# Experts ordered by load, three of them on 64 slots, in a two-layer encoder on one core

## The chip, the core and the metric

The kernel runs on one core of a Trainium2 chip. The core has a tensor engine (PE, with its weight loads shown apart as PEld), a vector engine (DVE), a scalar engine (ACT), GpSimd (POOL), and a sync engine (SP) on whose queue all the loads of weights are issued. The metric is device time of one execution in microseconds. A trace shows each instruction of one profiled execution, with times counted from the start of its span.

## The reference

Layer 0 is a convolution and pooling mixer, cross-attention and a dense SwiGLU; layer 1 is a Conformer convolution, cross-attention and the experts, on which this case turns. There are 256 tokens of 1024 features, 8 experts with 3584 hidden features, and each token takes its two best experts:

```python
def moe_swiglu(xn, router, w_gu, w_down):
    logits = (xn @ router).astype(jnp.float32)
    top_v, top_i = lax.top_k(logits, TOP_K)
    w = jax.nn.softmax(top_v, axis=-1)
    comb = jnp.sum(jax.nn.one_hot(top_i, N_EXPERTS, dtype=jnp.float32) * w[..., None],
                   axis=-2).astype(xn.dtype)
    out = jnp.zeros_like(xn)
    for e in range(N_EXPERTS):
        out = out + comb[..., e:e + 1] * swiglu(xn, w_gu[e], w_down[e])
    return out
```

With the reference's own inputs the experts get 68, 72, 52, 68, 57, 70, 76 and 49 tokens.

## The kernel before

All of layer 0, and layer 1 up to its attention, keep activations transposed; the change leaves them alone. Float32 products run as three passes of float32r: each operand is split into a high part (12 significant bits) and its remainder, here hi and lo, and hi x hi, lo x hi and hi x lo are summed in PSUM.

The experts run one after the other, in their natural order. `Gather` fills 128 slots with an expert's tokens: a one-hot tile made on DVE (`one_hot`), the tokens picked out by float32 products (`gathered`, L1008), and both parts of the result in `xg` (L1028 on ACT, L1029 on DVE). The slots are the stationary operand (128 columns), the weights move past them 512 columns at a time. The weights come in chunks of 128 x 2048 float32 (1 MB), 42 of them for each expert. `split` makes both parts of a chunk in two halves of 1024 columns: ACT writes hi (L161), DVE subtracts and writes lo (L162). There are four buffers of a half for hi and four for lo (NPART), so that the split runs at most two chunks ahead of PE.

An expert has seven steps (`j`). A step takes six chunks, called here A0 and A1 (the gate, `gate_up(j, 0)`), B0 and B1 (up, `gate_up(j, 1)`), and D0 and D1 (`down` of the step before; the last step's own two come at the expert's end). `moving` does twelve products of 512 columns with each chunk: hi of the weights with both parts of the slots (L204, L205: eight), then lo with the slots' hi (L209: four). `gate` applies SiLU to the gate's sum on ACT (L1076) and multiplies it with up's on DVE (L1078, tile `eh`); `to_rows` turns `eh` on PE (L1084) and splits it into `ht` (L1086 on ACT, L1087 on DVE). At an expert's end `weighted` splits the output (L1100, L1101) and `scatter` adds it to the tokens' rows (L1108, L1109 on PE, L1111 on DVE).

SP loads the chunks in the order of their use (`sources`, `fetch`), from addresses known when the kernel is built, into a ring of 17 slots: 11 `raw`, 6 `spare`. A load waits until the chunk that had the slot has been split. The order of the instructions on PE, ACT and DVE within the experts is set when the kernel is built, by a scheduler with its own estimate of times; each engine then executes its list strictly in that order, and waits where an operand isn't there. Slots beyond 128 would be done by a second pass under a branch (`overflow`), which is not entered.

Of the kernel before, what the change touches and what calls it, by code (L numbers as in the profile page):

```python
# [42 lines left out]
CAP = 128  # L43
TCKW = dict(schedule_with_timeline_sim=True)
# [3 lines left out]
RING = "rrrrrrrrsssssrrrrrs"   # the slots of the experts' chunks, later ones as their forerunners  # L48
# [3 lines left out]
G_TAPS = 4 * (11, 12)  # of the convolution's 31 taps, on GpSimd  # L52

# columns of the packed per-partition vectors
# [20 lines left out]
def _build(ctx, tc, io, cap):  # L75
# [32 lines left out]
    # ---------------------------------------------------------------- inputs and constants  # L108
# [21 lines left out]
    for _ in range(NWARM):       # the tensor engine's clock rises with its load  # L130
        PE.matmul(idle[:, :P], ones, ones, start=True, stop=True)
# [3 lines left out]
    # ---------------------------------------------------------------- helpers  # L135
# [36 lines left out]
    class Early:  # L172
        """The same in two whole chunks for use much later, split piece by piece."""
# [69 lines left out]
    def product_whole(raw, act):  # L243
        """The same with float32 operands as they are."""
# [19 lines left out]
    def split_whole(name, t):  # L264
        """The two parts of a whole operand."""
# [14 lines left out]
    def rsqrt(out, v, n):  # L280
        """out = v ** -0.5 for [128, n]: an estimate from the bits, then a step of the second
        order and one of the third."""
# [4 lines left out]
        def half(y):  # L287
            """t = -v * y ** 2 / 2"""
# [13 lines left out]
    class Sums:  # L302
        """Sums over features, by pairs of feature tiles as they come: on GpSimd, and the last
        `last` pairs on the tensor engine."""
# [19 lines left out]
        def pair(self):  # L324
            """Adds the last two summed tiles, or the halves of the only one."""
# [6 lines left out]
        def columns(self):  # L332
            """[128 tokens, 2]"""
# [10 lines left out]
    def rstd(sums):  # L344
        """The columns [128 tokens, 2] of 1 / rms."""
# [7 lines left out]
    def broadcast(cols, name="rb", tag="rb", bufs=1, scale=1.0):  # L353
        """[128, T] with cols[t] times scale in every partition."""
# [87 lines left out]
    # ---------------------------------------------------------------- cross-attention  # L442
# [72 lines left out]
    # ================================================================ layer 0: mixer  # L515
# [15 lines left out]
    # reciprocals of the window sizes, clipped at both ends of the sequence  # L531
# [34 lines left out]
    def pool_evac(j, ps):  # L566
# [9 lines left out]
        # window sums by doubling: s[i] = u[i] + ... + u[i + width - 1]  # L576
# [50 lines left out]
    # ================================================================ layer 0: attention, SwiGLU  # L627
# [73 lines left out]
    # ================================================================ layer 1: Conformer  # L701
# [102 lines left out]
    # LayerNorm over features: the mean (in every partition), then the centred variance; what is  # L804
    # kept is the negative of the centred activations
# [35 lines left out]
    # ================================================================ layer 1: attention  # L841
# [24 lines left out]
    class Tokens:  # L866
        """Tokens on partitions, a quarter of the features: the experts' input without the 1 / rms."""
# [24 lines left out]

    def sources():
        """The experts' chunks, as they are used."""
        for e in range(NE):
            for j in range(7):
                for i in range(4):
                    yield io["moe_gu"][e, j, i], 1
                    if i == 3 and j:
                        for n in range(2):  # L900
                            yield io["moe_down"][e, j - 1, n], 1
            for n in range(2):
                yield io["moe_down"][e, 6, n], 4 if e == NE - 1 else 1
# [30 lines left out]
    # ================================================================ layer 1: router  # L934
    ltri = work.tile([P, NE, NE], F32, tag="w1", name="ltri", bufs=w1b)    # 1 where the other expert comes first
# [7 lines left out]
    upper = work.tile([P, P], F32, tag="w1", name="upper", bufs=w1b)      # [t', t] = 1 where t' < t  # L943
# [35 lines left out]
    # a token's slot: how many earlier tokens chose the expert  # L979
# [7 lines left out]
    # ================================================================ layer 1: experts  # L987
    def one_hot(e, first, n, dt):
        oh = work.tile([P, 2, P], dt, tag="sqs", name="oh")
        for t in range(2):  # L990
# [354 lines left out]
```

## Time and profile before

| | us |
|---|---|
| median of three runs | 1596.82 (1596.51 to 1597.1) |
| span of the profiled execution | 1595.4 |
| what lies around the span, taken as median less span | 1.4 |
| experts, first weights to the last product's end | 593.3 to some 1579 |
| PE, DVE and ACT busy in those 985.7 us | 985.70, 892.44, 753.17 |

The profile page gives busy time by engine and by forty slices of the span, the costliest groups of instructions, and the chain that ended last. Time of a product in the trace runs from its start to its modelled end and overlaps the next one, so the distance between two starts tells what a product costs PE. For DVE and ACT likewise: a run of n equal instructions is shown with the time from the first's start to the last's end.

### The profile page before, as it was taken

The numbers are of one execution on the slowest core, as the hardware profiler recorded it, in microseconds if no ns is written. First come the engines' busy times: TensorE is split into PE (matmuls) and PEld (weight loads), VectorE is DVE, ScalarE is ACT, GpSimd is POOL, SyncE is SP. The second block draws the span as 40 slices with busy tenths as digits, with TensorE's granted clock in tenths as the row PEclk, the third lists the DMA queues.
The fourth block names the chain that finished last, engine by engine and source line by source line (L and its number), as shares of the span: only waits on it lengthen the run. The fifth ranks groups of instructions, "written<-read, shape, count | busy, mean of one in ns | idle before, by whom it ended". The sixth has DMA issues, their size and how long they took to land.

```text
span 1595.4 us, 23969 instructions
## 1 busy us (share of the span) xinstructions
PE 1569.4 (98%) x8978; PEld 1383.1 (87%) x8978; DVE 1346.2 (84%) x1723; ACT 1087.7 (68%) x1384; POOL 148.6 (9%) x206
## 2 busy tenths in 40 slices
PE   8899999999999999999999999999999999999996
PEld 8899999999889998888888888888888888888885
DVE  7866677766998769989989999989999989889896
ACT  5555554455576548777777777777777777777775
POOL 4710100000592110000000000000000000000000
PEclk9999999999999999999999999999999999999998
DMA  9654454336436569999999998998998999999950
GB/s 370 249 187 161 154 185 152 117 127 240 185 132 236 188 237 347 364 348 337 379 360 340 378 364 326 376 369 325 373 369 322 374 362 342 358 359 353 349 195 29
DMA packets 65213, 451.44 MB, mean 283 GB/s; under 512 B 7360, under 2 KB 7488, under 8 KB 12480
## 3 DMA queue, kind: packets, MB, share of 16 engines
q1 hardware_dynamic: 65088, 449.83, 75.4%
q8 instruction: 72, 1.18, 0.3%
q14 instruction: 53, 0.43, 0.1%
HBM read 448.75 MB, written 1.05 MB: 282 GB/s over the span
## 4 chain that ended last, share of the span: by engine, by line
PE 89%; POOL 3%; DVE 3%; ACT 2%; issue 1%; DMA 1%; SPq 0%; POOLq 0%; DVEq 0%; ACTq 0%
PE gu L209 13%; PE gu L204 13%; PE gu L205 13%; PE acc L198 6%; PE acc L197 6%; PE acc L196 6%; PE py L209 6%; PE py L204 6%; PE py L205 6%; POOL part L757 2%; PE gx L1008 2%; PE ht L1084 2%; DVE lo L162 1%; PE acc L248 1%; PE lead L197 1%
## 5 line engine op out<-in xcount | busy, mean ns | idle before, releaser
L162 DVE TENSOR_TENSOR lo<-raw,hi 128x1024 fp32r<-128x1024 f32 (+2 forms) x599 | 703.8, 1207 | 117.8 <-ACT hi L161 95.0
L161 ACT CAST hi<-raw 128x1024 fp32r<-128x1024 f32 (+2 forms) x599 | 600.3, 1033 | 266.6 <-PE acc L197 92.4
L204 PE MATMUL gu<-hi,xg 128*128 128x512 f32 x896 | 350.1, 391 | 0.0
L205 PE MATMUL gu<-hi,xg 128*128 128x512 f32 x896 | 349.3, 390 | 0.0
L162 DVE TENSOR_TENSOR lo<-spare,hi 128x1024 fp32r<-128x1024 f32 (+1 forms) x242 | 281.9, 1202 | 27.1 <-ACT hi L161 15.2
L161 ACT CAST hi<-spare 128x1024 fp32r<-128x1024 f32 (+1 forms) x242 | 241.6, 1038 | 55.3 <-PE gu L205 41.5
L209 PE MATMUL gu<-lo,xg 128*128 128x512 f32 x896 | 251.6, 391 | 0.0
L204 PEld LDWEIGHTS gu<-hi,xg 128*128 128x128 f32 x896 | 168.2, 188 | 35.3
L205 PEld LDWEIGHTS gu<-hi,xg 128*128 128x128 f32 x896 | 168.3, 188 | 35.2
L209 PEld LDWEIGHTS gu<-lo,xg 128*128 128x128 f32 x896 | 167.7, 188 | 35.6
L204 PE MATMUL py<-hi,ht 128*128 128x512 f32 x448 | 175.7, 394 | 0.0
L205 PE MATMUL py<-hi,ht 128*128 128x512 f32 x448 | 174.9, 390 | 0.0
L209 PE MATMUL py<-lo,ht 128*128 128x512 f32 x448 | 136.1, 396 | 0.0
L205 PEld LDWEIGHTS py<-hi,ht 128*128 128x128 f32 x448 | 84.2, 188 | 16.8
L204 PEld LDWEIGHTS py<-hi,ht 128*128 128x128 f32 x448 | 83.8, 188 | 16.4
L1236 POOL TENSOR_TENSOR fo<-accum,fn 128x512 f32<-128x512 f32 x2 | 2.5, 1269 | 995.1 <-DVE cnt L1255 995.1
L198 PE MATMUL acc<-a2h,lo 128*128 128x256 f32 x336 | 95.2, 283 | 0.0
L197 PE MATMUL acc<-a2l,hi 128*128 128x256 f32 x336 | 95.2, 283 | 0.0
L196 PE MATMUL acc<-a2h,hi 128*128 128x256 f32 x336 | 95.1, 283 | 0.0
L209 PEld LDWEIGHTS py<-lo,ht 128*128 128x128 f32 x448 | 81.8, 188 | 15.3
L196 PEld LDWEIGHTS acc<-a2h,hi 128*128 128x128 f32 x336 | 64.5, 192 | 0.0
L198 PEld LDWEIGHTS acc<-a2h,lo 128*128 128x128 f32 x336 | 64.5, 192 | 0.0
(371 smaller groups left out, 2639.5 us busy)
## 6 DMA issues: line engine op xcount, KB each, us to landing
raw<-in_moe_gu SPq DMA_DIRECT2D x139, 1024.0 KB, 6.1
spare<-in_moe_gu SPq DMA_DIRECT2D x85, 1024.0 KB, 6.3
raw<-in_moe_down SPq DMA_DIRECT2D x78, 1024.0 KB, 6.2
spare<-in_moe_down SPq DMA_DIRECT2D x32, 1024.0 KB, 5.4
raw<-in_ffn_gu SPq DMA_DIRECT2D x22, 1024.0 KB, 4.8
raw<-in_pw SPq DMA_DIRECT2D x12, 1024.0 KB, 4.8
raw<-in_ffn_down SPq DMA_DIRECT2D x16, 704.0 KB, 4.1
raw<-in_wk SPq DMA_DIRECT2D x8, 1024.0 KB, 7.0
```

The lines of the kernel that those rows point to most:

```text
L161: done[:] = (S.copy(hi[:, i:i + step], raw[:, a + i:a + i + step]), V.tensor_sub(lo[:, i:i + step], raw[:, a + i:a + i + step], f32(hi[:, ...
L162: V.tensor_sub(lo[:, i:i + step], raw[:, a + i:a + i + step], f32(hi[:, i:i + step])))
L196: PE.matmul(ps, a[0], b[0], start=first, stop=False)
L197: PE.matmul(ps, a[0], b[1], start=False, stop=False)
L198: PE.matmul(ps, a[1], b[0], start=False, stop=last)
L204: PE.matmul(ps, a[0], b[0], start=first and i == 0, stop=False)
L205: PE.matmul(ps, a[1], b[0], start=False, stop=False)
L209: ins = PE.matmul(ps, a[0], b[1], start=False, stop=last and i == n - 1)
L248: PE.matmul(ps[:, m, :], raw[:, m * 1024 + k * P:m * 1024 + (k + 1) * P], act(k), start=k == 0, stop=k == KD - 1)
L757: G.tensor_add(part, part, prod)
L1008: PE.matmul(px[:, kk * P:(kk + 1) * P], xt[:, t * D + d0:t * D + d0 + P], oh[:, t, :], start=t == 0, stop=t == 1)
L1084: PE.transpose(pt[:, i * P:(i + 1) * P], h[:, i * P:(i + 1) * P], ident)
```

## The change

The experts 1 to 7 are sorted by load on the chip, and the kernel then runs eight *positions*: position 0 is expert 0, positions 2, 4 and 6 (`NARROW`) take the three least loaded of the others, positions 1, 3, 5 and 7 the rest.

- The sort: loads by two products with ones (`pn`), ranks and permuted copies of the selection, slot and weight tables by some thirty small DVE instructions on 8 to 64 elements, 24 small memsets on GpSimd. SP reads the seven experts' numbers into registers (after the loads of position 0), and every later load of weights has an address from a register.
- A narrow position has 64 slots. The stationary operand's 128 columns hold 64 slots' hi and, beside them, the same slots' lo. A chunk then takes eight products of 512 columns (hi of the weights, then lo), and the sums of both halves of the output's rows are added afterwards: for the gate by two copies on ACT, an add on DVE and a SiLU, for `eh` and the output by the product that follows.
- In a narrow position B1 (one chunk in six) is not split: four float32 products take it as it is (`gate_up`, "gu == kh == 1"), and its ring slot is held until PE has read it.
- The test for the second pass is made at the start, by position, and the pass is under a branch for each position.

```diff
+    def slots(p):
+        return HALF if p in NARROW else cap
+    def side_by_side(dst, src):
+        v = dst.rearrange("p (k s n) -> p k s n", s=2, n=HALF)
+        src = src.rearrange("p (k n) -> p k n", n=HALF)
+        S.copy(v[:, :, 0, :], src)
+        V.tensor_sub(v[:, :, 1, :], src, f32(v[:, :, 0, :]))
...
+    def narrow(ps, xs, ws, first, last):
+        n = len(xs)
+        for part in range(2):
+            for i, (x, w) in enumerate(zip(xs, ws)):
+                ins = PE.matmul(ps, x, w[part], start=first and i == part == 0,
+                                stop=last and part == 1 and i == n - 1)
+        return ins
...
+                xs = [xg[:, k * P:(k + 1) * P] for k in range(kh * 4, kh * 4 + 4)]
+                if two and gu == kh == 1:
+                    w = whole_chunk()
+                    for kk in range(4):
+                        PE.matmul(pz, f32(xs[kk]), w[:, kk * 512:(kk + 1) * 512],
+                                  start=False, stop=kk == 3)
+                    continue
+                w = chunk()
+                ws = [w(kk * 512, (kk + 1) * 512) for kk in range(4)]
+                if two:
+                    narrow(pz, xs, ws, kh == 0, kh == 1)
+                    continue
...
-            S.activation(sg, pg, AF.Silu, scale=g.cw[:, 1:2])
+            if two:
+                S.copy(sg[:HALF], pg[HALF:])
+                S.copy(sg[HALF:], pg[:HALF])
+                V.tensor_add(sg, sg, pg)
+                S.activation(sg, sg, AF.Silu, scale=g.cw[:, 1:2])
...
+                for i in range(4):
+                    PE.matmul(pt[:, i * HALF:(i + 1) * HALF], h[:, i * P:(i + 1) * P], both,
+                              start=True, stop=True)
+                return side_by_side(ht[:, o:o + 512], pt[:, :4 * HALF])
...
+    V.tensor_tensor(place, across(rnk), down_(takes), op=ALU.is_equal)
+    def placed(dst, src):
+        m = square("match")
+        V.tensor_tensor(m, place, across(src), op=ALU.mult)
+        V.tensor_reduce(dst, m, axis=AX.X, op=ALU.add)
...
+        if e == 0:
+            ids += [nc.values_load(idi[0:1, p:p + 1], engines=(mybir.EngineType.SP,),
+                                   min_val=1, max_val=NE - 1) for p in range(1, NE)]
```

The scheduler makes new lists for PE, ACT and DVE out of it. The line numbers in the lists of the changed kernel are its own: there L169 makes lo, L168 hi, L1108 and L1124 are the narrow products (split and whole chunk), L1141 to L1144 the gate's copies, add and SiLU, L1148 is `eh`, L1157 turns it, L1039 and L1038 make `ht`. First DVE, a step in the middle of the fifth expert (position 4). Before:

```order
L1078 SCALAR_TENSOR_TENSOR eh<-gu,cw,esg 128x512
L162 TENSOR_TENSOR lo<-raw,hi 128x1024 x4
L1087 TENSOR_TENSOR ht<-ht 128x512
L162 TENSOR_TENSOR lo<-raw,hi 128x1024 x2
L162 TENSOR_TENSOR lo<-spare,hi 128x1024 x5
L1078 SCALAR_TENSOR_TENSOR eh<-gu,cw,esg 128x512
```

Now:

```order
L1148 SCALAR_TENSOR_TENSOR eh<-gu,cw,esg 128x512
L169 TENSOR_TENSOR lo<-spare,hi 128x1024
L169 TENSOR_TENSOR lo<-raw,hi 128x1024 x2
L1039 TENSOR_TENSOR ht<-ht 128x4x64
L169 TENSOR_TENSOR lo<-raw,hi 128x1024 x6
L1143 TENSOR_TENSOR esg<-esg,gu 128x512
L169 TENSOR_TENSOR lo<-raw,hi 128x1024
L1148 SCALAR_TENSOR_TENSOR eh<-gu,cw,esg 128x512
```

The nine halves between `eh` and the add are those of D0 (its second), D1, A0, A1 and B0; between the add and the next `eh` stands one half alone, the first of D0. In a step of position 2 the add stands later, after the halves of D0 and D1.

ACT at the same place, now:

```order
L1144 ACTIVATE esg<-esg,cw 128x512
L168 CAST hi<-raw 128x1024 x4
L1038 CAST ht<-ht 128x4x64
L168 CAST hi<-raw 128x1024 x6
L1141 COPY esg<-gu 64x512
L1142 COPY esg<-gu 64x512
L1144 ACTIVATE esg<-esg,cw 128x512
```

The SiLU stands behind the add of DVE and ahead of all four halves of D0 and D1.

PE there, now (the `py` are D0's and D1's sums):

```order
L1108 MATMUL gu<-lo,xg 128x512 x4
L1124 MATMUL gu<-raw,xg 128x512 x4
L1108 MATMUL py_11118<-hi,ht 128x512 x4
L1108 MATMUL py_11118<-lo,ht 128x512 x2
L1157 MATMUL ht<-kept,eh 128x64 x4
L1108 MATMUL py_11119<-hi,ht 128x512 x2
L1108 MATMUL py_11118<-lo,ht 128x512 x2
L1108 MATMUL py_11119<-hi,ht 128x512 x2
L1108 MATMUL py_11119<-lo,ht 128x512 x4
L1108 MATMUL gu<-hi,xg 128x512 x4
```

The whole chunk B1 follows B0 directly, and the turn of `eh` has moved forward into D0 and D1; before it stood in the next step's A0.

## Rows read from the trace of the kernel before

**Rows 1.** Page: busy time, share of the span and instructions by engine, then of the forty slices of the span PE's busy share and the granted clock, in tenths.

```profile
PE 1569.4 (98%) x8978; PEld 1383.1 (87%) x8978; DVE 1346.2 (84%) x1723; ACT 1087.7 (68%) x1384; POOL 148.6 (9%) x206
...
PE   8899999999999999999999999999999999999996
...
PEclk9999999999999999999999999999999999999998
```

**Rows 2.** The whole of the experts in one window: from:to in us, length, busy us and count of PE, PEld, DVE, ACT and POOL, granted clock, DMA share, GB/s.

```profile
593.30:1579.00 985.70, 985.70 (x4588) 819.86 (x4587) 892.44 (x865) 753.17 (x823) 0.00 (x0) 1.00 0.90 339
```

**Rows 3.** Timeline of PE within one chunk: start us, duration us, instruction.

```profile
660.01 0.39 PE L204 MATMUL gu<-hi,xg 128*128 128x512 f32 x1
660.23 0.39 PE L205 MATMUL gu<-hi,xg 128*128 128x512 f32 x1
660.46 0.61 PE L209 MATMUL gu<-lo,xg 128*128 128x512 f32 x2
660.91 0.39 PE L204 MATMUL gu<-hi,xg 128*128 128x512 f32 x1
```

**Rows 4.** Timeline of ACT, the SiLU of two steps that follow each other.

```profile
894.84 0.68 ACT L1076 ACTIVATE esg<-gu,cw 128x512 f32<-128x512 f32 x1
...
911.63 0.68 ACT L1076 ACTIVATE esg<-gu,cw 128x512 f32<-128x512 f32 x1
```

**Rows 5.** Timeline of PE, float32 products as they are: those of 256 columns in the Conformer, those of 128 that gather tokens. Each product is recorded as two instructions.

```profile
398.31 31.89 PE L248 MATMUL acc<-a,raw 128*128 128x256 f32 x147
...
589.71 3.82 PE L1008 MATMUL gx<-oh,xt 128*128 128x128 f32 x32
```

**Rows 6.** Timeline of DVE in a step of the fourth expert and in one of the last expert (from 1488.84 on).

```profile
899.73 0.75 DVE L1078 SCALAR_TENSOR_TENSOR eh<-gu,cw,esg 128x512 f32<-128x512 f32 x1
900.40 4.69 DVE L162 TENSOR_TENSOR lo<-raw,hi 128x1024 fp32r<-128x1024 f32 x4
...
1488.84 0.68 DVE L1087 TENSOR_TENSOR ht<-ht 128x512 fp32r<-128x512 f32 x1
1489.44 4.79 DVE L162 TENSOR_TENSOR lo<-raw,hi 128x1024 fp32r<-128x1024 f32 x4
1496.64 2.36 DVE L162 TENSOR_TENSOR lo<-spare,hi 128x1024 fp32r<-128x1024 f32 x2 [2.41 <-ACT hi L161]
```

**Rows 7.** Timeline of ACT in that step of the last expert.

```profile
1494.98 0.69 ACT L1076 ACTIVATE esg<-gu,cw 128x512 f32<-128x512 f32 x1 [2.52 <-PE gu L209]
1495.57 1.99 ACT L161 CAST hi<-spare 128x1024 fp32r<-128x1024 f32 x2
```

**Rows 8.** Groups by line and form: count, busy us, mean ns of one, idle time before them.

```profile
L162 DVE TENSOR_TENSOR lo<-raw,hi 128x1024 fp32r<-128x1024 f32 x563 | 672.7, 1229 | 103.4 <-ACT hi L161 80.7 <-PE py L209 13.4 <-PE gu L209 5.8
...
L1086 ACT CAST ht<-ht 128x512 fp32r<-128x512 f32 x56 | 32.6, 582 | 23.7 <-PE ht L1084 23.7
...
L1111 DVE TENSOR_TENSOR accum<-accum,so 128x512 f32<-128x512 f32 x32 | 21.0, 680 | 2.0 <-PE so L1109 2.0
```

**Rows 9.** Loads: what SP's queue waited for in all (us, times, longest), then windows as in Rows 2, two of the experts' and one near the start.

```profile
SPq L140 <- DVE lo L162: 1062.1, 362, 15.0
...
720.00:760.00 40.00, 40.00 (x182) 33.03 (x181) 36.63 (x37) 31.31 (x33) 0.00 (x0) 1.00 0.91 337
760.00:800.00 40.00, 40.00 (x185) 33.16 (x184) 36.38 (x34) 31.27 (x34) 0.00 (x0) 1.00 0.98 377
20.00:40.00 20.00, 18.00 (x148) 17.54 (x147) 17.95 (x35) 10.10 (x16) 11.48 (x13) 1.00 1.02 421
```

**Rows 10.** Timeline of DVE in the router, two instructions on 64 to 128 elements and one on 16; timeline of POOL ahead of it; the registers' load at the end of the program (minimum, median and longest in ns).

```profile
587.20 0.29 DVE L967 TENSOR_REDUCE rank<-gt 128x16 f32<-128x128 f32 x1
587.52 0.17 DVE L969 TENSOR_SCALAR sel<-rank 128x16 f32<-128x16 f32 x1
...
492.29 0.56 POOL L829 CAST p2h<-cv 128x256 fp32r<-128x256 f32 x1 [11.80 <-ACT cv L828]
...
L1258 SPq TENSOR_LOAD <-over x1: 472/472/472, 1582.4 to 1582.4; - x1
```

**Rows 11.** The clock: windows as in Rows 2, then the timeline of PE around the wait in the first of them.

```profile
62.60:69.40 6.80, 2.74 (x10) 2.37 (x11) 6.80 (x12) 2.20 (x4) 4.22 (x4) 0.56 0.47 154
35.00:40.00 5.00, 4.11 (x36) 4.06 (x35) 5.00 (x14) 3.06 (x6) 1.52 (x2) 1.00 1.03 426
...
58.31 0.28 PE L197 MATMUL acc<-a0l,hi 128*128 128x256 f32 x1
58.43 0.28 PE L198 MATMUL acc<-a0h,lo 128*128 128x256 f32 x1
...
67.03 1.22 PE L591 MATMUL pool<-pm,ch 128*128 128x256 f32 x2 [4.06 <-POOL pm L586]
...
69.12 0.41 PE L196 MATMUL acc<-memgh,hi 128*128 128x256 f32 x1
69.33 0.41 PE L197 MATMUL acc<-memgl,hi 128*128 128x256 f32 x1
```

More of the change, by code (lines that the diff above doesn't have):

```diff
@@ L43 @@
 CAP = 128
+NARROW = (2, 4, 6)
+WIDE = (1, 3, 5, 7)
+HALF = CAP // 2
 TCKW = dict(schedule_with_timeline_sim=True)
@@ L891, in _build, with weights @@
     wos = [load(io["wo"][1, c]) for c in range(4)]
+    ids = [0]
+    def weights(name, p, *at):
+        if p == 0:
+            return io[name][(0, *at)]
+        return io[name][(bass.ds(ids[p], 1), *at)].rearrange("e p c -> (e p) c")
     def sources():
@@ L932, in _build @@
     r5(3, product(None, tiles_of(at.o), w=split(wos[3])))
-    ltri = work.tile([P, NE, NE], F32, tag="w1", name="ltri", bufs=w1b)
+    kept = work.tile([P, T + 16], F32, tag="w1", name="kept", bufs=w1b)
+    ltri = kept[:, :NE * NE].rearrange("p (e q) -> p e q", e=NE)
     V.memset(ltri, 0.0)
@@ L1019, in step @@
             if j == 3:
-                self.oh = one_hot(self.e, 0, cap, F32)
+                self.oh = one_hot(self.e, 0, slots(self.e), F32)
             else:
@@ L1029, in rows, with rows_narrow @@
                 V.tensor_sub(lo, px, f32(hi))
+        def rows_narrow(self):
+            px = tr_tile("gx")
+            for k in range(KD):
+                for t in range(2):
+                    PE.matmul(px[:, k * HALF:(k + 1) * HALF],
+                              xt[:, t * D + k * P:t * D + (k + 1) * P],
+                              self.oh[:, t, :HALF], start=t == 0, stop=t == 1)
+            side_by_side(xg[:, :D], px)
         def turn(self):
@@ L1053, in _build, with whole_chunk, chunk @@
     ht = big_tile("ht", F32R)
-    def chunk(pieces=2):
+    def whole_chunk():
         if not ahead:
             fetch()
-        return split(ahead.popleft(), pieces=pieces)
+        return ahead.popleft()
+    def chunk(pieces=2):
+        return split(whole_chunk(), pieces=pieces)
+    def narrow(ps, xs, ws, first, last):
[5 more added lines that the diff above has]
+        return ins
     def expert(e, g, following):
@@ L1062, in expert @@
         py = out_tiles()
+        two = e in NARROW
         def gate_up(j, gu):
@@ L1066, in gate_up @@
             for kh in range(2):
-                with nullcontext():
-                    w = chunk()
+                xs = [xg[:, k * P:(k + 1) * P] for k in range(kh * 4, kh * 4 + 4)]
[10 more added lines that the diff above has]
+                    continue
                 moving(pz, [(xg[:, k * P:(k + 1) * P], xg[:, D + k * P:D + (k + 1) * P])
                             for k in range(kh * 4, kh * 4 + 4)],
-                       [w(kk * 512, (kk + 1) * 512) for kk in range(4)], kh == 0, kh == 1)
+                       ws, kh == 0, kh == 1)
             return pz
@@ L1091, in down @@
             o = (j % 2) * D
+            if two:
+                return narrow(py[n], [ht[:, o + f * P:o + (f + 1) * P] for f in range(4)],
+                              [w(f * 512, (f + 1) * 512) for f in range(4)], j == 0, j == 6)
             return moving(py[n],
@@ L1161, in _build, with columns_of @@
     V.reciprocal(den, den)
-    weights = V.tensor_tensor(comb[:, :, :, 0], ex, den[:, :, None].to_broadcast([P, 2, NE]),
-                              op=ALU.mult)
+    V.tensor_tensor(comb[:, :, :, 0], ex, den[:, :, None].to_broadcast([P, 2, NE]), op=ALU.mult)
+    combn = comb
     g.step(5)
+    pn = tr_tile("pn")
+    PE.matmul(pn[:, :NE], ones, sel[:, 0, :], start=True, stop=False)
+    PE.matmul(pn[:, :NE], ones, sel[:, 1, :], start=False, stop=True)
+    def columns_of(t, *widths):
+        ends = np.cumsum(widths).tolist()
+        return [t[:, b - w:b] for b, w in zip(ends, widths)]
@@ new lines, in _build @@
+    cnt, rnk, takes, limit, eight, idf, load_, both, place = columns_of(
+        kept[:, NE * NE:], *[NE] * 7, HALF, NE * NE)
+    seln, posn, combn = columns_of(
+        work.tile([P, 8 * NE], F32, tag="w1", name="placed", bufs=w1b), 2 * NE, 2 * NE, 4 * NE)
+    seln, posn = (v.rearrange("p (t e) -> p t e", t=2) for v in (seln, posn))
+    combn = combn.rearrange("p (t e w) -> p t e w", t=2, e=NE)
+    place = place.rearrange("p (q e) -> p q e", q=NE)
+    for r, p in enumerate((0, *NARROW, *WIDE)):
+        G.memset(takes[:, p:p + 1], float(r))
+        G.memset(limit[:, p:p + 1], float(slots(p)))
@@ new lines, in _build, with square, across, down_ @@
+    for e in range(NE):
+        G.memset(eight[:, e:e + 1], float(e))
+    V.tensor_copy(cnt, pn[:, :NE])
+    V.memset(cnt[:, 0:1], -1.0)
+    def square(name):
+        return work.tile([P, NE, NE], F32, tag="w1", name=name, bufs=w1b)
+    def across(v):
+        return v[:, None, :].to_broadcast([P, NE, NE])
+    def down_(v):
+        return v[:, :, None].to_broadcast([P, NE, NE])
+    less, same = square("less"), square("same")
+    V.tensor_tensor(less, across(cnt), down_(cnt), op=ALU.is_lt)
@@ new lines, in _build @@
+    V.tensor_tensor(same, across(cnt), down_(cnt), op=ALU.is_equal)
+    V.tensor_tensor(same, same, ltri, op=ALU.mult)
+    V.tensor_add(less, less, same)
+    V.tensor_reduce(rnk, less, axis=AX.X, op=ALU.add)
+    V.tensor_copy(cnt[:, 0:1], pn[:, 0:1])
+    V.tensor_tensor(place, across(rnk), down_(takes), op=ALU.is_equal)
[3 more added lines that the diff above has]
+        V.tensor_reduce(dst, m, axis=AX.X, op=ALU.add)
@@ new lines, in _build @@
+    for t in range(2):
+        placed(seln[:, t, :], sel[:, t, :])
+        placed(posn[:, t, :], pos[:, t, :])
+        placed(combn[:, t, :, 0], comb[:, t, :, 0])
+        V.tensor_copy(combn[:, t, :, 1], comb[:, t, :, 1])
+    placed(idf, eight)
+    placed(load_, cnt)
+    idi = small.tile([P, NE], I32, tag="idi", name="idi", bufs=1)
+    V.tensor_copy(idi, idf)
+    V.tensor_sub(load_, load_, limit)
+    most = small.tile([P, 1], F32, tag="most", name="most")
+    V.tensor_reduce(most, load_, axis=AX.X, op=ALU.max)
@@ L1165, in _build @@
+    over = small.tile([P, 1 + NE], I32, tag="over", name="over", bufs=1)
+    V.tensor_single_scalar(over[:, :1], most, 0.5, op=ALU.is_gt)
+    V.tensor_single_scalar(over[:, 1:], load_, 0.5, op=ALU.is_gt)
+    V.tensor_add(both, ident[:, :HALF], ident[:, HALF:])
     for e in range(NE):
@@ L1182, in overflow @@
         for t in range(2):
-            PE.matmul(pc[:, 0:2], oh[:, t, :], comb[:, t, e, :], start=t == 0, stop=t == 1)
+            PE.matmul(pc[:, 0:2], oh[:, t, :], combn[:, t, e, :], start=t == 0, stop=t == 1)
         cw = small.tile([P, 2], F32, tag="cw", name="cw")
@@ L1192, in overflow @@
                 for kh in range(2):
-                    w = load(io["moe_gu"][e, j, gu * 2 + kh])
+                    w = load(weights("moe_gu", e, j, gu * 2 + kh))
                     for kk in range(4):
@@ L1209, in overflow @@
             for n in range(2):
-                w = load(io["moe_down"][e, j, n])
+                w = load(weights("moe_down", e, j, n))
                 for f in range(4):
@@ L1250, in _build @@
     finish()
-    pn = psE.tile([P, 512], F32, tag="py", name="pn")
-    PE.matmul(pn[:, :NE], ones, sel[:, 0, :], start=True, stop=False)
-    PE.matmul(pn[:, :NE], ones, sel[:, 1, :], start=False, stop=True)
-    cnt = small.tile([P, 1], F32, tag="cnt", name="cnt")
-    V.tensor_reduce(cnt, pn[:, :NE], axis=AX.X, op=ALU.max)
-    over = small.tile([P, 1], I32, tag="over", name="over", bufs=1)
-    V.tensor_single_scalar(over, cnt, cap + 0.5, op=ALU.is_gt)
     flag = nc.values_load(over[0:1, 0:1], min_val=0, max_val=1)
@@ L1260, in _build @@
         for e in range(NE):
-            overflow(e)
+            more = nc.values_load(over[0:1, 1 + e:2 + e], min_val=0, max_val=1)
+            with tc.If(more > 0):
+                overflow(e)
         finish()
```

24 lines of the change are left out of this document (15 added, 9 removed).

## The prediction

> **What bounds the kernel now.** I read the page's busy times first, then the window of the experts, then single steps. PE is busy in 98% of the span and in all 985.7 us of the experts, at a granted clock of 1.00; DVE has 93 us to spare there, ACT 233, POOL does nothing [rows 1, 2]. A split product of 512 columns costs PE 0.227 us from start to start: its duration, 0.39, overlaps the next one [rows 3]. A step is six chunks of twelve products, 72 x 0.227 = 16.3, and the turn of `eh`; measured are 911.63 - 894.84 = 16.79 [rows 4]. DVE's twelve halves at 1.15 to 1.17 with `eh` and `ht` come to some 15.2 of it [rows 6], which leaves it 1.5. Loads wait for DVE to give back ring slots, not PE for loads: SP's queue stands 1062 us on `lo`, and 337 to 377 GB/s in the experts face 421 near the start [rows 9]. So the experts end when PE has gone through its columns, and fewer columns are time won until the next engine binds.
>
> **What a narrow step costs PE.** The trace has no such step; its prices come from neighbours. Five split chunks take 8 x 0.227 = 1.81 each instead of 2.72, together 9.07. The chunk that is used as it is has four products of two records each. A record of 256 columns costs 31.89/147 = 0.217, one of 128 columns 3.82/32 = 0.119 [rows 5]; so 512 columns are 0.434 by the first, 0.476 by the second, and 0.227 if a record cost no more than a product of split operands. The chunk is 3.47, 3.81 or 1.81. I take 3.47, as the nearest in columns; that record already costs at 256 columns what a split product does at 512, which speaks against the low end. The turn, eight short products at 0.12 as the 128 columns of [rows 5], is 0.95. Sum 13.5, against 16.79: 3.3 per step if PE alone sets the pace.
>
> **What it costs DVE and ACT.** DVE makes ten halves instead of twelve; four in a row take 4.69 or 4.79, 1.15 to 1.17 start to start once the last one's tail is off [rows 6]. With `eh` 0.67 (899.73 to 900.40), the add at about 0.6 and `ht` on half the columns at about 0.45, its step is 13.2. ACT gains two copies of 64 x 512, unseen in the trace; the nearest rows are 0.58 for a copy out of PSUM and 0.68 for an add [rows 8]. It loses two casts at 1.0 each [rows 7] and has 24% to spare, so they count only where they stand in a chain.
>
> [...]
>
> **The order makes a loop.** In position 4 DVE's list is: `eh`, three halves, `ht`, six halves (A0 to B0), add, one half of D0, `eh`. ACT's SiLU waits for that add and stands ahead of all casts of D0 and D1, so DVE can't start them early. `eh` waits until PE is through B1, and B1, 3.47 long, comes behind B0, whose last products need DVE's sixth half. From `eh` to `eh`: `eh` 0.67, nine halves 10.35, `ht` 0.45, what PE has left of B0 after its last half (two products and the way there) 0.55, B1 3.47, hand-offs 0.25. **15.74**, against 16.79: 1.05 saved per step, not 3.3. Hand-offs: ACT's first cast ends near 1495.57 + 1.0, DVE's half starts at 1496.64, 0.07 later [rows 6, 7]; a product ends 0.39 - 0.227 = 0.16 after the next one starts [rows 3]. Such a place exists already: in the last expert the SiLU waits 2.52 for PE, and DVE 2.41 for the casts behind it [rows 6, 7], while PE stays busy; there the split chunks ahead cover it. For the same reason wide steps stay at 16.8 even where the lists around them change.
>
> Position 6 has that order too; in position 2 the add stands behind the halves of D0 and D1 in the middle steps, which therefore run at PE's own pace, 13.5 to 13.7: 3.1 saved each.
>
> **The sum.** Seven steps of an expert are five in full, an entry and an exit.
> - Limited steps: five in position 4, five in position 6, two in position 2: 12 x 1.05 = 12.6. Free steps: 3 x 3.1 = 9.3.
> - Entries, from the old expert's last B1 to the new one's second B1. The old D chunks, gather and scatter stay. Wide: eight chunks 21.76 + turn 0.43. Narrow: three chunks 5.44 and one whole 3.47, then 0.25 + 0.67 + four halves 4.6 + 0.55 + 3.47. 22.19 - 18.45 = 3.7; three are 11.1.
> - Exits: four D chunks, 4 x (2.72 - 1.81) = 3.6; I leave off 0.7, one eviction of 512 columns [rows 8], since the sum of the halves is a new link between `eh` and the output. Three are 8.7.
> - The sort, about thirty small DVE instructions during position 0, at 0.29 for 64 to 128 elements and 0.17 for 16 [rows 10]: 22 x 0.29 + 10 x 0.17 = 8. DVE has 1.5 to spare per step there while PE is busy, so most of it is hidden; between 0 and 8, I take -1.5.
> Together 41.7 - 1.5 = 40. The profiled execution's 1595.4 becomes 1555.2, and with the 1.4 around it, which I leave as it is, **1557**.
>
> **What I cost at nothing.** The 24 memsets lie in POOL's idle 11.8 us before 492.29 [rows 10]; without that cover, 24 short ones would delay `p2h`. SP's seven register loads cost some 0.5 each (the one in the trace 0.472), with their moves perhaps 6 us; they stand behind position 0's loads, and the ring then holds up to 17 chunks, of which PE uses one in 2.8 us. Without that lead they would cost all 6. Later loads get about one more instruction on SP, which waits most of the time anyway [rows 9]. B1's slot is held longer, until PE is through: about two chunks of 17. The test for the second pass is made while PE is busy; the branches at the end of a position are one more instruction per engine, under 0.5 each by that register load, too small for a term of its own. No expert of the reference beyond 128 tokens exists, so no pass is taken for wide ones.
>
> **Rivals.**
> - *The orders cost more* (0.15): position 2 is limited too (3 x 2 = 6), and the halves come at 1.22, as long as one lasts (15 x 9 x 0.05 = 7): 1570. For it: waits in the lists tend to add up where ACT and DVE alternate. Against it: the rows of four halves in a run.
> - *The orders don't bind* (0.08): `eh` doesn't wait as I read it, or the whole chunk is nearer 1.81. Then PE sets the pace: 15 x 3.2 + 3 x 3.9 + 8.7 = 68, less 1.5: 1530.
> - *The loads bind* (0.04). 336 chunks less about 13 fetched ahead are 323 from 593 on. At the experts' present mean of 339 GB/s a chunk takes 3.09, and the last lands at 1591, no gain; at the 377 of the window from 760 on [rows 9] it is 2.78 and 1491, no bound. The middle, 358, gives 2.93, 1540, and with about 22 for the last chunks and the output 1562. Against it: the wait of loads on `lo`, and 421 GB/s at 20 to 40 us.
> - *Slower: the clock falls* (0.09). In narrow positions PE waits for the first time, some 2 us per step. At 62 to 69 us PE was busy 2.74 of 6.80, and the granted clock 0.56; the same products then came at 0.21 instead of 0.12 after a wait of 4.06 [rows 11]. Against it: 4.11 of 5 busy at 35 to 40 us kept 1.00. A step of 13.5 at half the clock lasts 27, 11 more than the limited one. From four such steps on the gain is gone, with seven of the 21 it is 1557 + 77 = 1634; the end at no change is 0.03 of the 0.09.
> - *It doesn't do what it says* (0.02). If a narrow position had over 64 tokens, its second pass would run: 42 chunks at 3.47 = 146 us or more. By the reference's loads the least three of experts 1 to 7 are 49, 52 and 57.
>
> [...]
>
> **How the numbers follow.** The forecast, 1546 to 1567 by the bounds of the whole chunk (15 x 0.34 = 5 more), the sort (1.5 less, 6.5 more) and the free steps, has 0.62. With the orders that cost more, half the case of free orders and the loads, 1538 to 1580 holds over 0.8. A measurement of this kernel can tell about 0.2%, 3.2 us, from no change. Faster: 0.62 + 0.15 + 0.08 + 0.04 = 0.89; same 0.03, from the clock; slower 0.06 + 0.02 = 0.08.
>
> **What would show it.** Starts of `eh` 15.7 apart in positions 4 and 6, and about 13.6 in the middle of position 2; PE waiting there for `lo` some 2 us a step, DVE for ACT's casts and for PE before `eh`; the whole chunk's records 0.434 apart; wide steps still 16.8; position 0's length, against the first expert's now, shows the sort's price. The forecast is wrong if the steps are near 13.5 throughout (the orders), at or above 16.4 (order or loads: PE's wait then names `lo` or the load), if the granted clock in a narrow position is under 1.00, or if PE waits on loads.

## The result

The changed kernel takes 1550.52 us (median of four runs, 1549.56 to 1551.01), the kernel before beside it 1596.96: a ratio of 0.9709, 95% interval 0.9695 to 0.9722, 46.4 us less. Forecast were 1557 and 40 less. The profiled execution has a span of 1549.3, 46.1 under the one of before.

The page of the changed kernel, busy time by engine:

```profile
PE 1513.3 (98%) x8558; PEld 1295.2 (84%) x8558; DVE 1298.1 (84%) x1730; ACT 1052.1 (68%) x1381; POOL 149.0 (10%) x230
```

The granted clock stands at nine tenths or more in all forty slices but the last, as before. Against [rows 1] PE lost 56 us of busy time and the span 46: PE now waits. Where it does, the windows show (columns as in [rows 2]): all the experts, position 2 from its first `eh` to 946, a piece of position 4.

```profile
593.30:1533.00 939.70, 929.88 (x4176) 732.04 (x4175) 844.71 (x877) 717.71 (x822) 0.00 (x0) 1.00 0.92 356
...
854.20:946.00 91.80, 90.95 (x401) 67.30 (x400) 83.98 (x89) 74.93 (x91) 0.00 (x0) 1.00 1.01 414
...
1100.00:1160.00 60.00, 56.86 (x222) 37.39 (x222) 50.06 (x52) 46.03 (x55) 0.00 (x0) 1.00 1.00 404
```

In position 2 PE is still busy nearly all the time, in position 4 it isn't, at a granted clock of 1.00 in both. The loads moved 414 GB/s in that window of position 2 (413 up to the first `eh` of position 3), more than in any experts' window of [rows 9].

From one position's first `eh` to the next one's, worked out from the starts of `eh` on DVE in the two traces:

| stretch | before | after | difference |
|---|---|---|---|
| span's start to the first `eh` | 606.4 | 608.5 | +2.1 |
| position 0 (wide) | 124.1 | 123.3 | -0.8 |
| position 1 (wide), entry to 2 | 123.9 | 122.4 | -1.5 |
| position 2 (narrow) | 123.9 | 105.6 | -18.3 |
| position 3 (wide) | 123.9 | 119.4 | -4.5 |
| position 4 (narrow) | 123.9 | 115.6 | -8.3 |
| position 5 (wide) | 123.3 | 119.3 | -4.0 |
| position 6 (narrow) | 123.9 | 115.0 | -8.8 |
| position 7 (wide) to the span's end | 122.2 | 120.2 | -2.1 |

The three narrow positions are alike in work, yet position 2 gave twice what 4 and 6 gave. A wide position that follows a narrow one gains too. The narrow one's last D chunks aren't the reason: on PE they end ahead of the wide position's first `eh` (in position 2 near 944, `eh` at 959.8). But in the new lists more of the wide position's own products stand ahead of that `eh`: in position 3 PE then makes 38 products of 512 columns up to the second `eh` where it made 49 (counted in the two traces, give or take one), in 9.2 us instead of 11.8. In positions 3 and 5 another 1.5 lie in the entry to the next narrow one. DVE in a middle step of position 2, from `eh` to `eh` (start, duration, instruction, idle time before it):

```profile
876.68 0.75 DVE L1148 SCALAR_TENSOR_TENSOR eh<-gu,cw,esg 128x512 f32<-128x512 f32 x1 [0.72 <-ACT esg L1144]
877.35 5.77 DVE L169 TENSOR_TENSOR lo<-raw,hi 128x1024 fp32r<-128x1024 f32 x5
883.03 0.42 DVE L1039 TENSOR_TENSOR ht<-ht 128x256 fp32r<-128x256 f32 x1
883.37 4.62 DVE L169 TENSOR_TENSOR lo<-raw,hi 128x1024 fp32r<-128x1024 f32 x4
887.90 0.69 DVE L1143 TENSOR_TENSOR esg<-esg,gu 128x512 f32<-128x512 f32 x1
888.50 1.22 DVE L169 TENSOR_TENSOR lo<-raw,hi 128x1024 fp32r<-128x1024 f32 x1
890.13 0.75 DVE L1148 SCALAR_TENSOR_TENSOR eh<-gu,cw,esg 128x512 f32<-128x512 f32 x1 [0.40 <-ACT esg L1144]
```

ACT between the gate's copies and the next casts there:

```profile
886.53 2.94 ACT L168 CAST hi<-raw 128x1024 fp32r<-128x1024 f32 x3
889.38 0.72 ACT L1144 ACTIVATE esg<-esg,cw 128x512 f32<-128x512 f32 x1
```

By the order in which PE takes the chunks, two of the four halves at 883.37 are B0's and two D0's; D1's first stands between the add and `eh`, its second behind `eh`. So on DVE the add stands behind D0's halves, and not behind those of D0 and D1, as the section on the change has it. On ACT the three casts at 886.53 are D1's two and one of the next A0, so that all four casts of D0 and D1 come ahead of the SiLU.

Then DVE, ACT and PE in a step of position 4:

```profile
1104.49 0.75 DVE L1148 SCALAR_TENSOR_TENSOR eh<-gu,cw,esg 128x512 f32<-128x512 f32 x1 [0.73 <-PE gu L1124]
1105.16 1.22 DVE L169 TENSOR_TENSOR lo<-spare,hi 128x1024 fp32r<-128x1024 f32 x1
...
1108.90 6.89 DVE L169 TENSOR_TENSOR lo<-raw,hi 128x1024 fp32r<-128x1024 f32 x6
1115.70 0.68 DVE L1143 TENSOR_TENSOR esg<-esg,gu 128x512 f32<-128x512 f32 x1
1118.11 1.22 DVE L169 TENSOR_TENSOR lo<-spare,hi 128x1024 fp32r<-128x1024 f32 x1 [1.72 <-ACT hi L168]
1120.06 0.75 DVE L1148 SCALAR_TENSOR_TENSOR eh<-gu,cw,esg 128x512 f32<-128x512 f32 x1 [0.73 <-PE gu L1124]
```

```profile
1114.35 0.59 ACT L1141 COPY esg<-gu 64x512 f32<-64x512 f32 x1 [1.56 <-PE gu L1108]
1114.94 0.58 ACT L1142 COPY esg<-gu 64x512 f32<-64x512 f32 x1
1116.42 0.72 ACT L1144 ACTIVATE esg<-esg,cw 128x512 f32<-128x512 f32 x1 [0.90 <-DVE esg L1143]
1117.05 1.98 ACT L168 CAST hi<-spare 128x1024 fp32r<-128x1024 f32 x2
```

```profile
1116.42 3.60 PE L1124 MATMUL gu<-raw,xg 128*128 128x512 f32 x8
```

Here is the loop of the forecast: DVE ends B0's last half at 1115.70, PE starts the whole chunk at 1116.42, ACT idles 0.90 for the add, DVE 1.72 for the cast behind the SiLU and 0.73 for PE, and `eh` follows at 1120.06: 15.57 after the one before it. In position 2 the same work, with those casts ahead of the SiLU, took 890.13 - 876.68 = 13.45. The chain that ended last runs through PE there; its pieces (start, us, engine, line, instructions) show the whole chunk's eight records and a turn of `eh`:

```profile
872.96 3.43 PE gu L1124 x8
...
880.03 0.84 PE ht L1157 x8
```

### The profile page after: what moved, and what is told of

Same layout as the page of the kernel before. It is cut to its first block, busy times and chain, and to the rows that moved or that the text cites. A ratio compares the mean times of both kernels' runs of the same rounds, so it can differ in the third digit from the quotient of the medians.

```text
span 1549.3 us, 23644 instructions
## 1 busy us (share of the span) xinstructions
PE 1513.3 (98%) x8558; PEld 1295.2 (84%) x8558; DVE 1298.1 (84%) x1730; ACT 1052.1 (68%) x1381; POOL 149.0 (10%) x230
## 3 DMA queue, kind: packets, MB, share of 16 engines
q8 instruction: 69, 1.13, 0.3%
HBM read 448.75 MB, written 1.05 MB: 290 GB/s over the span
## 4 chain that ended last, share of the span: by engine, by line
PE 81%; DVE 9%; POOL 3%; issue 3%; ACT 2%; DMA 1%; SPq 0%; DVEq 0%; POOLq 0%; ACTq 0%
PE gu L211 8%; PE gu L212 8%; PE gu L216 8%; PE acc L205 7%; PE acc L204 7%; PE acc L203 7%; DVE lo L169 7%; PE gu L1124 5%; PE gu L1108 4%; PE py L211 4%; PE py L216 4%; PE py L212 4%; PE py L1108 3%; POOL part L764 2%; PE gx L1027 1%
## 5 line engine op out<-in xcount | busy, mean ns | idle before, releaser
L169 DVE TENSOR_TENSOR lo<-raw,hi 128x1024 fp32r<-128x1024 f32 (+3 forms) x573 | 671.0, 1208 | 120.1 <-ACT hi L168 110.4
L168 ACT CAST hi<-raw 128x1024 fp32r<-128x1024 f32 (+3 forms) x573 | 565.6, 1031 | 213.5 <-PE acc L204 92.0
L169 DVE TENSOR_TENSOR lo<-spare,hi 128x1024 fp32r<-128x1024 f32 (+1 forms) x226 | 261.4, 1203 | 24.6 <-ACT hi L168 20.5
L168 ACT CAST hi<-spare 128x1024 fp32r<-128x1024 f32 (+1 forms) x226 | 221.5, 1036 | 23.6 <-PE gu L212 11.9
L211 PE MATMUL gu<-hi,xg 128*128 128x512 f32 x560 | 218.8, 391 | 0.0
L212 PE MATMUL gu<-hi,xg 128*128 128x512 f32 x560 | 218.4, 390 | 0.0
L216 PE MATMUL gu<-lo,xg 128*128 128x512 f32 x560 | 154.2, 391 | 0.7 <-DVE lo L169 0.7
L216 PEld LDWEIGHTS gu<-lo,xg 128*128 128x128 f32 x560 | 104.7, 188 | 23.9 <-DVE lo L169 1.9
L211 PEld LDWEIGHTS gu<-hi,xg 128*128 128x128 f32 x560 | 105.1, 188 | 22.2 <-ACT hi L168 0.2
L212 PEld LDWEIGHTS gu<-hi,xg 128*128 128x128 f32 x560 | 105.1, 188 | 21.8
L211 PE MATMUL py<-hi,ht 128*128 128x512 f32 x280 | 111.1, 398 | 0.0
L212 PE MATMUL py<-hi,ht 128*128 128x512 f32 x280 | 109.3, 390 | 0.0
L1108 PE MATMUL gu<-lo,xg 128*128 128x512 f32 x252 | 80.3, 411 | 8.0 <-DVE lo L169 8.0
L216 PE MATMUL py<-lo,ht 128*128 128x512 f32 x280 | 84.0, 395 | 0.0
L1108 PE MATMUL gu<-hi,xg 128*128 128x512 f32 x252 | 71.2, 396 | 0.0
L1108 PEld LDWEIGHTS gu<-lo,xg 128*128 128x128 f32 x252 | 43.4, 188 | 31.6 <-DVE lo L169 25.2
```

The costliest lines, as they stand in the source:

```text
L168: done[:] = (S.copy(hi[:, i:i + step], raw[:, a + i:a + i + step]), V.tensor_sub(lo[:, i:i + step], raw[:, a + i:a + i + step], f32(hi[:, ...
L169: V.tensor_sub(lo[:, i:i + step], raw[:, a + i:a + i + step], f32(hi[:, i:i + step])))
L211: PE.matmul(ps, a[0], b[0], start=first and i == 0, stop=False)
L212: PE.matmul(ps, a[1], b[0], start=False, stop=False)
L216: ins = PE.matmul(ps, a[0], b[1], start=False, stop=last and i == n - 1)
L1108: ins = PE.matmul(ps, x, w[part], start=first and i == part == 0, stop=last and part == 1 and i == n - 1)
```

## The experiments

The theory: in positions 4 and 6 the order of the lists on ACT and DVE sets the step, not the work. The main rival: the work, or loads (B1 holds its slot of the ring longer), sets it. All ratios are against the kernel before.

**Order alone, forwards.** For narrow positions the chunks of D0 and D1 are split ahead of the gate, and the SiLU is queued behind their last cast:

```diff
+            if two and j:
+                for n in range(2):
+                    ws[n] = chunk()
+                behind = done[0]
+            h = gate(pg, pu, behind)
...
+                with late(behind):
+                    S.activation(sg, sg, AF.Silu, scale=g.cw[:, 1:2])
```

> Only the order on ACT and DVE changes: in every narrow step the SiLU stands behind the last cast of D0 and D1 instead of ahead of them. Order theory: the steps of positions 4 and 6, 15.57 apart now, come down to PE's own 13.4 to 13.9, as the four middle steps of position 2 already are; with ten such steps and the last of position 2, 11 x 1.9 = 21 us less: 1526 to 1534. Rival (loads and ring: B1's slot is held until PE has read it, so that positions 4 and 6 wait for weights): the order is not what binds, 1548 to 1552.

In the code `late(behind)` queues an instruction behind that cast on ACT. Measured 1544.79 (1544.02 to 1545.12), 0.9672 (0.9656 to 0.9688). Six us less than the changed kernel: neither the 1526 to 1534 of the theory nor unchanged. The steps of positions 4 and 6 went to 15.2, not 13.5. DVE in one of them:

```profile
1103.79 2.35 DVE L169 TENSOR_TENSOR lo<-raw,hi 128x1024 fp32r<-128x1024 f32 x2
1107.37 0.42 DVE L1039 TENSOR_TENSOR ht<-ht 128x256 fp32r<-128x256 f32 x1 [1.23 <-ACT ht L1038]
1108.31 4.63 DVE L169 TENSOR_TENSOR lo<-raw,hi 128x1024 fp32r<-128x1024 f32 x4 [0.52 <-ACT hi L168]
...
1113.79 2.36 DVE L169 TENSOR_TENSOR lo<-spare,hi 128x1024 fp32r<-128x1024 f32 x2 [0.24 <-ACT hi L168]
```

The wait behind the SiLU is gone, and another has taken its place: with the edit, `ht` stands after two halves instead of three, before PE has turned `eh`, and A1's casts queue behind it on ACT. 1.23 + 0.52 + 0.24 = 2.0 idle per step, on a DVE that has 13.2 of work.

**And that wait too.** The same, with `ht`'s cast and subtraction queued behind the halves of A1:

```diff
+                with late(done[0] if two else None), late(done[1] if two else None):
+                    to_rows(j - 1, h)
```

> The SiLU behind all casts of D0 and D1 as before, and ht's cast and subtraction queued behind the halves of A1, where ACT and DVE no longer meet them before PE has turned eh. Theory (the order of the lists, one wait after the other): the 1.2 us in which DVE waits for ht and the 0.5 behind it go, steps of positions 4 and 6 fall from 15.2 to 13.4 to 13.9, 10 x 1.5 = 15 us below the kernel with the SiLU moved alone: 1527 to 1534. Rival (once the SiLU is out of the way, loads are what binds at about 420 GB/s, six chunks in 15): steps stay at 15.0 to 15.2, 1542 to 1546.

Measured 1531.28 (1530.79 to 1531.81), 0.9587 (0.9571 to 0.9603): within the 1527 to 1534 of the theory. Three of the five steps of positions 4 and 6 take 13.5 to 13.7, as it had them; the other two don't, at 15.2 and 14.3. In the first of these two the gather for the next expert stands in the lists, and in position 4 DVE waits 2.11 in it for PE's `pc`. DVE in one of the three, in position 4:

```profile
1114.62 0.75 DVE L1152 SCALAR_TENSOR_TENSOR eh<-gu,cw,esg 128x512 f32<-128x512 f32 x1
1115.29 4.62 DVE L169 TENSOR_TENSOR lo<-raw,hi 128x1024 fp32r<-128x1024 f32 x4
1119.83 0.42 DVE L1039 TENSOR_TENSOR ht<-ht 128x256 fp32r<-128x256 f32 x1
1120.16 2.35 DVE L169 TENSOR_TENSOR lo<-raw,hi 128x1024 fp32r<-128x1024 f32 x2
1122.48 0.69 DVE L1146 TENSOR_TENSOR esg<-esg,gu 128x512 f32<-128x512 f32 x1
1123.55 2.36 DVE L169 TENSOR_TENSOR lo<-raw,hi 128x1024 fp32r<-128x1024 f32 x2 [0.38 <-ACT hi L168]
1125.83 2.35 DVE L169 TENSOR_TENSOR lo<-spare,hi 128x1024 fp32r<-128x1024 f32 x2
1128.10 0.75 DVE L1152 SCALAR_TENSOR_TENSOR eh<-gu,cw,esg 128x512 f32<-128x512 f32 x1
```

13.48 from `eh` to `eh`, 0.38 of it idle, and PE busy throughout; the loads kept up with 421 GB/s:

```profile
1090.00:1130.00 40.00, 40.00 (x164) 28.75 (x164) 38.65 (x40) 33.89 (x41) 0.00 (x0) 1.00 1.01 421
```

So loads don't set the 15.57, nor does B1's slot. They aren't far off, though: six chunks of 1.05 MB in 13.48 us are 467 GB/s, more than the 421 that came, so by this estimate such a step also uses up some of the chunks that were loaded ahead. This version beats both kernels, 19.2 us under the changed one, with the same arithmetic.

**Half of it.** As the last, but only D0 is split ahead of the gate, so D1's halves stay behind the SiLU.

```diff
-                for n in range(2):
-                    ws[n] = chunk()
+                ws[0] = chunk()
```

> As the last one, but the SiLU goes behind the casts of D0 only, so that D1's halves come after eh. Theory: the loop runs from eh (0.67) over six halves (6.9), ht 0.45 and B0's two halves (2.3) to B0's rest 0.55 and B1's 3.43, with 0.25 of hand-offs: 14.5 a step in positions 4 and 6, 10 x 1.05 = 10 us under the changed kernel: 1538 to 1543. Rival (loads): 15.0 and more, 1544 to 1547.

Measured 1540.47 (1539.54 to 1541.2), 0.9644 (0.9628 to 0.966), steps of 14.49 in positions 4 and 6, but for the one with the gather (16.2). DVE, the end of one:

```profile
1126.71 2.36 DVE L169 TENSOR_TENSOR lo<-raw,hi 128x1024 fp32r<-128x1024 f32 x2
1130.54 0.75 DVE L1152 SCALAR_TENSOR_TENSOR eh<-gu,cw,esg 128x512 f32<-128x512 f32 x1 [1.47 <-PE gu L1124]
```

The loop was worked out as 14.5 from its members, and `eh` waits 1.47 on DVE for PE's whole chunk, as it should if D1's two halves wait on the other side of `eh`.

**Order alone, backwards.** D0's and D1's splits are queued behind the SiLU in every narrow position, up to the expert's own last two.

```diff
-            w = chunk(4 if e == NE - 1 and j == 6 else 2)
+            with tc.issue_after(silu[0].ins) if two and j < 6 else nullcontext():
+                w = chunk(4 if e == NE - 1 and j == 6 else 2)
```

> The reverse: the casts of D0 and D1 are queued behind the SiLU in all narrow steps, so position 2 gets the order that positions 4 and 6 have by themselves. Order theory: its four middle steps rise from 13.5 to about 15.3 (eh 0.67, eight halves 9.2, ht 0.45, then add 0.6, SiLU 0.9, a cast 1.0 and two halves 2.4 in one chain), the others stay: 7 us more, 1556 to 1560. Rival (loads and ring): unchanged, 1549 to 1552.

Measured 1555.54 (1554.54 to 1556.63), 0.9737 (0.972 to 0.9753); positions 4 and 6 as before the edit, position 2's middle steps 14.75 instead of 13.5, where 15.3 was expected. DVE:

```profile
888.09 0.68 DVE L1145 TENSOR_TENSOR esg<-esg,gu 128x512 f32<-128x512 f32 x1
890.50 2.36 DVE L169 TENSOR_TENSOR lo<-raw,hi 128x1024 fp32r<-128x1024 f32 x2 [1.72 <-ACT hi L168]
892.78 0.74 DVE L1150 SCALAR_TENSOR_TENSOR eh<-gu,cw,esg 128x512 f32<-128x512 f32 x1
```

The same 1.72 as in position 4, brought about by the order alone. The loop's members had been added up to 15.2; from 878.02, the `eh` before, to 892.78 they took 14.76, both the part up to the add and the part behind it being shorter than put. The total is half a microsecond under the lower end of what was expected.

**B1 split.** The condition `gu == kh == 1` becomes `gu == kh == 2`, which never holds; the narrow positions split all six chunks.

> B1 is split like the other five chunks in the narrow positions. Theory: PE would need 6 x 1.81 + 0.84 = 11.7 a step, DVE 12 x 1.15 + 0.67 + 0.6 + 0.4 = 15.5, so DVE binds in all three positions: positions 4 and 6 stay at 15.5 to 15.7, position 2 loses its 13.5 (4 x 2 = 8 us): 1557 to 1563. Rival (the float32 chunk's 3.43 on PE is what positions 4 and 6 pay for): they fall by 1.6 a step, PE's saving, 10 x 1.6 = 16 less, with position 2 as now: 1533 to 1538.

Measured 1566.02 (1563.22 to 1566.17), 0.9799 (0.9782 to 0.9815). DVE binds, at 15.2 to 15.8 for most narrow steps, and position 2 loses its advantage; the rival (PE's saving comes through) is out by over 25 us. 1566 is 3 above what was expected. The entries to positions 2 and 4 (last `eh` to first `eh`) grew from 25.9 to 29.3, which the expectation didn't have. The whole chunk is worth 15 us as the lists stand, though it makes PE slower by 1.6 a step; what part of the 15 is the clock, which falls in this kernel, no run separates. Windows in position 4 (columns as above) and PE in them:

```profile
1096.00:1101.00 5.00, 4.51 (x20) 2.99 (x20) 5.00 (x7) 4.94 (x8) 0.00 (x0) 1.00 1.01 354
1101.00:1106.00 5.00, 3.67 (x11) 2.87 (x11) 5.00 (x6) 3.69 (x5) 0.00 (x0) 0.73 0.99 365
```

```profile
1102.43 1.38 PE L1108 MATMUL py<-hi,ht 128*128 128x512 f32 x4 [1.33 <-DVE ht L1039]
...
1104.46 1.91 PE L1108 MATMUL py<-hi,ht 128*128 128x512 f32 x4
1106.16 0.87 PE L1108 MATMUL py<-lo,ht 128*128 128x512 f32 x2
1106.87 0.62 PE L1108 MATMUL gu<-hi,xg 128*128 128x512 f32 x2
```

After a wait of 1.33 for `ht` the granted clock was 0.73 in the window, and four products took 1106.16 - 1104.46 = 1.70 instead of 0.91; from 1106.87 on they came at the old pace. The twelve products from 1102.43 on took 4.4 us instead of 2.7: PE lost 1.7. DVE was busy throughout, so that this loss cost the kernel as much isn't shown. The clock fell three times in this trace. PE's waits for `ht` from 840 on (us in all, times, longest):

```profile
PE py L1108 <- DVE ht L1039: 2.7, 2, 1.3
PE gx L1027 <- DVE ht L1039: 1.9, 1, 1.9
```

Each of the three was followed by a stretch with a granted clock of 0.51: 864.3 to 867.7 (wait of 1.33 up to 863.66), 949.6 to 953.1 (1.93 up to 948.73), and 1103.2 to 1106.7, the one above. In the 5 us before each, PE was busy 3.5, 3.1 and 3.5. PE's other waits from 840 on reached 0.7; in the windows from 1110 to 1166 and from 1300 to 1420 the granted clock was 1.00, with waits of up to 0.40 between 1130 and 1160.

**The whole chunk elsewhere.** A1 in place of B1.

```diff
-                if two and gu == kh == 1:
+                if two and gu == 0 and kh == 1:
```

> The float32 chunk is A1, the gate's second, instead of B1. PE's and DVE's work are the same. Order theory: the long products no longer stand between the last half of B0 and eh, and two or three casts stand ahead of the SiLU, so the loop opens: steps of 13.4 to 14.2 in all narrow positions, 10 x 1.6 = 16 less: 1529 to 1538. Rival (the work, not its place, sets 15.57): 1548 to 1552.

Measured 1567.5 (1566.75 to 1569.25), 0.9817 (0.9801 to 0.9834). 17 us slower than the changed kernel; the theory's expectation was wrong by 29 us or more, and the rival's by 15, both to the same side. Steps of 16.93 in positions 4 and 6; ACT and PE in one:

```profile
1118.60 0.58 ACT L1141 COPY esg<-gu 64x512 f32<-64x512 f32 x1 [4.90 <-PE gu L1124]
...
1119.79 2.00 ACT L168 CAST hi<-raw 128x1024 fp32r<-128x1024 f32 x2
```

```profile
1114.96 3.59 PE L1124 MATMUL gu<-raw,xg 128*128 128x512 f32 x8
1117.99 1.48 PE L1108 MATMUL gu<-hi,xg 128*128 128x512 f32 x4
...
1120.89 0.73 PE L1108 MATMUL gu<-hi,xg 128*128 128x512 f32 x2 [0.50 <-ACT hi L168]
```

I had looked only at the loop through `eh`. The gate's copies now wait 4.90 for the long products, and B1's casts stand behind the copies on ACT, so PE comes to B1 before its halves do. The rival as stated (work, not place: unchanged) falls with the miss: the work is the same and the time isn't.

**What the sort costs.** No narrow position, all else kept: `NARROW = ()`.

> The sort, the registers and the addresses from registers stay, but every position has 128 slots and splits every chunk. It prices what the change adds. Theory: the sort's DVE instructions cost 1 to 2 us in position 0 and nothing else does: 1597.5 to 1599.5. Rival (each load with an address from a register costs SP's queue time that PE ends up waiting for, or the sort's eight us are all on the path): 1601 to 1606.

Measured 1597.17 (1596.3 to 1597.83), 0.9999 (0.9989 to 1.0008). Sort, registers and addresses cost nothing that can be told, and the 1 to 2 us that the expectation gave the sort don't show (1597.17 is 0.3 under its lower end); the second position's first `eh` starts at 730.7 against 730.5 before.

**Addresses known when built**, in the order that these inputs give, and no registers.

> The changed kernel, but the loads' addresses are known when it is built (the order that the reference's inputs give), with no registers; the sort of the tables stays. Theory: SP has nothing on the path, 1549.5 to 1551.5. Rival (registers and their moves cost): 1543 to 1548.

Measured 1550.61 (1550.22 to 1551.49), 0.9709 (0.9693 to 0.9725), the changed kernel's own time.

## Why the prediction was right, and where its sizes were off

Direction, bound and mechanism hold; of 40.2 us forecast for the profiled execution 46.1 came. By the prediction's own steps:

- *PE's price of a narrow step.* The float32 chunk takes 3.43 for its eight records, 0.43 each, where 3.47 was taken from 256 columns. The turn is 0.84 for 0.95. With 9.07 for the five split chunks that is 13.3 instead of 13.5.
- *DVE's.* Six halves lie between 1108.90 and 1115.70, 1.13 each, where 1.15 was taken. The second run of four in [rows 6], 4.79 long, gives 1.19 once its last half's 1.23 is taken off, not the 1.17 that the prediction read. One such instruction lasts 1.229 in the mean of [rows 8] and 1.22 at 1105.16 here; no run shows that as the distance of halves in a row. The 16.4 that the prediction sets as a limit for a step is its loop with nine halves at 1.22 instead of 1.15: 15.74 + 9 x 0.07.
- *The loop.* Forecast 15.74, measured 15.57, and wide steps stayed at 16.8. The waits are where they were said to be: the SiLU on the add, DVE on the cast behind it, `eh` on the whole chunk. Position 2's middle steps ran at PE's pace as forecast, though the list was misread in part: on DVE the add stands behind D0's halves alone there, and it is the SiLU on ACT that stands behind all four casts of D0 and D1. Four experiments moved it by the order alone, to 15.2, 14.49 and, in three steps of five, 13.5 in positions 4 and 6, and to 14.75 in position 2. The mark "PE waits some 2 us a step for `lo`" was not what the profile shows: its waits come to 0.2 to 0.4 at a time, some 0.9 a step (PE is busy 14.71 of the 15.56 from 1104.50 to 1120.06), though by distances its work is 13.3. The rest is drawn as busy time of the products, whose ends are modelled. DVE's idle 1.72 + 0.73 is the better mark. PE's waits for `lo` in the narrow positions (us in all, times, longest):

```profile
PE gu L1108 <- DVE lo L169: 8.0, 33, 0.4
```

- *The step that was mis-sized* is the sum over narrow steps: 12.6 + 9.3 = 21.9 forecast, 28.4 measured (five intervals of `eh` in each of three positions: 6.6, 6.6 and 15.25). Position 2 has four free steps, not three; its step 1, which I counted as limited by the order, took 14.04. Free steps saved 3.5, not 3.1 (13.5 against a mean of 17.0). And limited steps saved 1.31 instead of 1.05: the loop came 0.17 shorter, and I had set it against 16.79, the plain step, while one of the five also holds the gather for the next expert, 17.51 before and 15.89 after.
- *Entries, exits and sort*: 18.3 forecast together, 17.7 measured (46.1 less 28.4). That is nearer than the parts are. From the last `eh` of one position to the second of the next, the three entries gave 11.9 (11.1 forecast) and the three exits 6.7 (8.7 forecast); the rest, -0.9, holds the later first `eh` and small shifts in wide positions. The sort was put at 1.5 of a range 0 to 8; alone it costs nothing that can be told. In the changed kernel the first `eh` comes 2.1 later and position 0 makes up 0.8, which would fit 1.3; but the first `eh` of the nine kernels with the sort comes anywhere from 606.8 to 609.1, so that such a difference can't be laid to it.
- *Costed at nothing*: SP's registers. Seven loads of 0.262 in 3.4 us after position 0's, where some 0.5 each and 6 with their moves were put, and the kernel without them is no faster.

```profile
L1317 SPq TENSOR_LOAD <-idi x7: 262/262/279, 663.8 to 667.2; - x7
```

- *Rivals.* Orders that don't bind (1530): wrong for the kernel as its lists stand; the 1531 of the reordered version comes near that price, though not all of its steps are free. Orders that cost more (1570): the halves came at 1.13, not 1.22, and position 2 stayed free. Loads: 414 GB/s in position 2 and no wait of PE on a load. The clock: it stayed at 1.00 in the narrow positions here, but the rival was real; in the kernel with B1 split it fell three times to 0.51, behind waits of 1.33 to 1.93, for some 3.5 us each.

## What to carry to other kernels

When a change takes work off the engine that binds, look at the lists of the other engines before counting the gain: an instruction that waits for a partner and stands ahead of independent work closes a loop. The loop's members, added up from the trace, gave the step within 0.2 us twice (15.74 for 15.57, 14.5 for 14.49) and were 0.5 off once (15.2 for 14.75); where one looked at the wrong loop, the sum was of no use (13.4 to 14.2 for 16.93). Take the order apart wait by wait, since removing one wait showed the next (1550.5, then 1544.8, then 1531.3). Moving a long operation "elsewhere" means asking anew who waits for it and what is queued behind that.

## What was not expected

- The place of a float32 chunk among six, with equal work, is worth 17 us (B1 1550.5, A1 1567.5).
- In the kernel with B1 split the granted clock fell behind each of three single waits of PE (1.33, 1.93 and 1.33 us) and stayed at 0.51 for some 3.5 us; behind the waits of 0.2 to 0.4 in the changed kernel's positions 4 and 6, several in a step, it stayed at 1.00.
- Loads from register addresses, seven eighths of the experts' weights, cost nothing against fixed ones (1550.52 and 1550.61).
